# Moving weights placed 64 bytes in front of the stationary operand, modulo 512

## Chip, cores and metric

The kernel runs on one core of one Trainium2 chip. The metric is the device time of one execution in microseconds; lower is better. Before the change three runs took 756.55, 757.05 and 758.76 us, a median of 757.05 us.

## What is computed

The reference is a decoder trunk of two layers over 256 tokens of width 1024, in float32. Layer 0 mixes with a dilated sliding-window attention, layer 1 with a forgetting attention, and each is followed by a SwiGLU feed-forward net (FFN). Cut to what matters here:

```python
h = h + dilated_mixer(rmsnorm(h, g_a), w_in_a, w_out_a)     # w_in: 1024 x 9216, w_out: 1024 x 1024
h = h + swiglu(rmsnorm(h, g_f0), w_gu[0], w_down[0])        # w_gu: 1024 x 5632, w_down: 2816 x 1024
h = h + forgetting_mixer(rmsnorm(h, g_b), w_in_b, b_f, w_out_b)   # w_in: 1024 x 3088
h = h + swiglu(rmsnorm(h, g_f1), w_gu[1], w_down[1])
return rmsnorm(h, g_final)

def swiglu(h, w_gu, w_down):
    gu = h @ w_gu
    g, u = gu[..., :D_FF], gu[..., D_FF:]
    return (silu(g) * u) @ w_down
```

## The kernel before

Each float32 operand of the large products is kept as a pair of rounded float32r parts, high and low (`wh`/`wl` for weights, two halves of `xt` for the normalised activations, `oth`/`otl` for the attention's output, `ah`/`al` for the FFN's gated activations). `mm3` (L179 and L184) makes one product of three matmuls: high times high, high times low, low times high. TensorE keeps one operand still (the stationary one, 128 columns, loaded by LDWEIGHTS) and streams the other (the moving one, 256 or 512 columns). In the profile a matmul row names its operands as output <- moving, stationary, and "128x256" or "128x512" is the moving width.

Weights come as pieces of 128 x 2048. `piece` reads each by two DMAs into `raw` tiles, and `split` writes `wh` by ScalarE (L73) and `wl` by VectorE (L75). Both tags have four buffers in turn. The order of the pieces is the list `order`, and two further pieces are always under way. A piece is used in one of two ways:

- As the stationary operand: `proj_feat`, used for the queries and keys of both mixers (`a_in`, `b_in` with w of 0 or 1) and for the FFN's up projections (`gu`) from f = 3 on. The moving operand is `xt`, 256 columns. One `proj_feat` is 8 steps of `mm3`, so 24 matmuls; one FFN piece (`up(f)`) is 48.
- As the moving operand: `proj_tok` (256 columns; the stationary operand is `xt`) for some values and for the FFN's first three `gu` pieces, the "head" of `ffn`; `proj_pair` (512 columns; `xt` is stationary) for the other values and the very first piece, which is written out in the lead loop (L366); `out_proj` (512 columns; `oth`/`otl` are stationary) with the `a_out` and `b_out` pieces; and `down` (512 columns; `ah`/`al` are stationary) with the `dn` pieces. With `narrow`, `mm3` cuts its second and third matmul into two of 256 columns, so that the next group follows sooner.

In the FFN's main loop two `up(f)` (96 matmuls) alternate with one `down` for both halves of the tokens: 22 matmuls of 512 columns and 4 of 256. One `dn` piece of each layer (f index `LATE`) stands in the tiles of `oth`/`otl` and not in `wh`/`wl`.

Where a tile starts in its partition of SBUF follows from the pools' order and sizes. A `wh` or `wl` buffer has 8192 bytes, 16 times 512, and all other sizes between are such that in the built program every one of them starts at byte 352 modulo 512. A tile of 448 bytes named `gap`, never written, stands ahead of `xt`, which so starts at 288. `ah`, `al`, `oth` and `otl` start at 352. All steps within these tiles that matmuls take are multiples of 512 bytes, so what counts modulo 512 is the same for each matmul of a kind:

| moving <- stationary | where | matmuls | moving minus stationary, modulo 512 |
|---|---|---|---|
| `xt` <- `wh`/`wl`, 256 wide | `proj_feat` | 3360 | -64 |
| `wh`/`wl` <- `xt`, 256 wide | `proj_tok`, narrow ends of `proj_pair` | 500 | +64 |
| `wh`/`wl` <- `xt`, 512 wide | `proj_pair`, lead loop | 278 | +64 |
| `wh`/`wl` <- `oth`/`otl`, 512 wide | `out_proj` | 192 | 0 |
| `wh`/`wl` <- `ah`/`al`, 512 wide | `down` | 438 | 0 |
| `wh`/`wl` <- `ah`/`al`, 256 wide | narrow ends of `down` | 84 | 0 |
| `oth`/`otl` <- `ah`/`al` | `down` of the piece `LATE` | 52 | 0 |

The matmuls are counted in the built program; the offsets are worked out from its addresses.

Of the kernel before, what the change touches and what calls it, by code (L numbers as in the profile page):

```python
# [11 lines left out]
F32R = mybir.dt.float32r  # L12
# [4 lines left out]
P = 128  # L17
# [14 lines left out]
def trunk(ctx: ExitStack, tc: tile.TileContext, T, out):  # L32
    nc = tc.nc

    cst = ctx.enter_context(tc.tile_pool(name="cst", bufs=1))
    wp = ctx.enter_context(tc.tile_pool(name="wp", bufs=1))
# [5 lines left out]
    def first():  # L42

        return tc.high_priority(offset=300)
# [25 lines left out]
    def split(pair, view, src, early=True, after=None):  # L70
        hi, lo = pair
        with first() if early else nullcontext():
            a = nc.scalar.activation(view(hi), src, AF.Copy)  # L73
            with tc.issue_after(after.ins) if after else nullcontext():
                return a, nc.vector.tensor_tensor(view(lo), src, view(hi).bitcast(F32), op=ALU.subtract)  # L75


    def piece(key, todo=None):
        if key[0][:2] == "dn" and key[1] == LATE:
            wh, wl = (y.rearrange("p k c -> p (k c)") for y in fm_tile("ot", KT, 1))  # L80
        else:
            wh, wl = (wp.tile([P, 2048], F32R, tag=y, name=y, bufs=4) for y in ("wh", "wl"))
        for c in range(2):
            raw = wp.tile([P, 1024], F32, tag="raw", name="raw", bufs=5)
            u = slice(c * 1024, (c + 1) * 1024)
            nc.sync.dma_start(raw, T[key[0]][key[1]][:, u])
            cut = lambda after=None, raw=raw, u=u: split((wh, wl), lambda y: y[:, u], raw, False, after)
            if todo is None:
                cut()
            else:  # L90
                todo.append(cut)
        return wh, wl

    def fm_tile(tag, n, bufs):
        return tuple(ap.tile([P, n, S], F32R, tag=f"{tag}{x}", name=f"{tag}{x}", bufs=bufs) for x in "hl")
# [34 lines left out]
    def weights(nm, i, after=None):  # L130

        upto = order.index((nm, i)) + AHEAD
        while state["next"] <= min(upto, len(order) - 1):
            key = order[state["next"]]
            cuts = []
            ready[key] = piece(key, cuts)
            for cut in cuts:
                cut(after)
            state["next"] += 1
        return ready.pop((nm, i))  # L140
# [187 lines left out]
    def in_order(cut):  # L328

        after = ExitStack()  # L330
        for y in cut:
            after.enter_context(tc.issue_after(y.ins))
        return after
# [6 lines left out]
    def square(i):  # L340
        return nc.scalar.activation(part[i].rearrange("p (j s) -> p j s", s=S), xs[i], AF.Square, scale=D ** -0.5)

    def plus(a, b):
        return nc.vector.tensor_tensor(a, a, b, op=ALU.add)

    cut = []
    for k in range(KT):
        if k % 4 == 0:
            w = tuple(wp.tile([P, 2048], F32R, tag=y, name=y, bufs=4) for y in ("wh", "wl"))
        g, u = g_a[:, k:k + 1], slice(k % 4 * 512, k % 4 * 512 + 512)  # L350
        with first(), in_order(cut):
            if k == 0:
                a = nc.vector.tensor_scalar(hi[:, k], xk[k], g, None, op0=ALU.mult)
            else:
                a = nc.scalar.activation(hi[:, k], xk[k], AF.Copy, scale=g)
            b = nc.vector.scalar_tensor_tensor(lo[:, k], xk[k], g, hi[:, k].bitcast(F32), op0=ALU.mult,
                                               op1=ALU.subtract)
            with in_order((a, b)):
                cut = split(w, lambda y: y[:, u], wk[k])
        if k in (1, 5, 7):  # L360
            with first(), in_order(cut):
                a = [square(i) for i in {1: (0, 1), 5: (2,), 7: (3,)}[k]][-1]
                cut = (a, plus(part[0], part[1]) if k == 1 else cut[1])
        for y, z in ((0, 0), (1, 0), (0, 1)):
            for t in range(2):
                nc.tensor.matmul(lead[t], xt[y][:, k, t * P:(t + 1) * P], w[z][:, u], start=k + y + z == 0,  # L366
                                 stop=k == KT - 1 and z == 1)
    cuts = []
    ready[order[1]] = w
    ready[order[2]] = piece(order[2], cuts)  # L370
    ready[order[3]] = piece(order[3], cuts)
    state["next"] = 4
    with first(), in_order(cut):
# [682 lines left out]
```

## Time and profile before

| | |
|---|---|
| runs | 756.55, 757.05, 758.76 us; median 757.05 us |
| profiled execution | span 757.5 us from its first to its last instruction; what lies around the span is not listed for it |
| PE (TensorE's matmuls) busy | 747.3 us, 99% |
| PEld (weight loads, beside PE) busy | 689.3 us, 91% |
| DVE (VectorE) busy | 500.0 us, 66% |
| ACT (ScalarE) busy | 381.7 us, 50% |
| POOL (GpSimd) busy | 56.9 us, 8% |
| mean granted TensorE clock | 0.998 |

The duration that the profile gives a matmul holds its way through the array; the next matmul starts long before it is over. How fast matmuls follow each other is read from the timeline, as the time from a matmul's start to that of the next, or over a stretch as the difference of two starts divided by the number of matmuls between. A stretch of equal matmuls without a wait in it gives the pace of that kind.

### The profile page before, as it was taken

The page shows a single profiled execution, that of the slowest core. Times are in us where ns is not written, and L with a number is a line of the kernel's source. Part 1 is how long each engine was busy: PE and PEld are TensorE (multiplying, and loading weights), DVE is VectorE, ACT ScalarE, POOL GpSimd, SP SyncE. Part 2 cuts the span into 40 slices and gives each one's busy share as a digit, 9 for nine tenths or more (in the row PEclk, how much of TensorE's full clock was granted, in tenths as well). Part 3 has the DMA queues.
Part 4 walks back from the last instruction along what each step waited for, and adds up shares of the span by engine and source line. Part 5 has one row for each costly group of instructions (what it writes and reads, how often), then busy time and mean ns, then how long its engine had stood idle before and what let it go on. Part 6 is the DMA issues. An engine that isn't in the chain of part 4 may idle for free.

```text
span 757.5 us, 14562 instructions
## 1 busy us (share of the span) xinstructions
PE 747.3 (99%) x6018; PEld 689.3 (91%) x6018; DVE 500.0 (66%) x760; ACT 381.7 (50%) x628; POOL 56.9 (8%) x99
## 2 busy tenths in 40 slices
PE   9999999999999999999999999999999999999996
PEld 7998989999988899999999988999889999999995
DVE  7987977877878466545456473887756645456533
ACT  7635437446346455444454454587645444455521
POOL 0600003004013000000000013000000000000000
PEclk9999999999999999999999999999999999999999
DMA  9965553653655267565667454634326665556601
GB/s 333 301 194 168 167 178 127 206 186 115 195 174 195 77 218 248 178 207 180 196 215 233 135 167 140 223 112 151 129 85 220 225 200 190 192 198 209 209 2 55
DMA packets 38355, 135.04 MB, mean 178 GB/s; under 512 B 4369, under 2 KB 5777, under 8 KB 38289
## 3 DMA queue, kind: packets, MB, share of 16 engines
q1 hardware_dynamic: 38144, 134.01, 53.5%
q8 instruction: 47, 0.77, 0.4%
q14 instruction: 20, 0.16, 0.1%
q10 hardware_dynamic: 144, 0.10, 0.0%
HBM read 133.05 MB, written 1.05 MB: 177 GB/s over the span
## 4 chain that ended last, share of the span: by engine, by line
PE 90%; DMA 2%; ACT 2%; issue 2%; DVE 2%; POOL 1%; SPq 0%; POOLq 0%; DVEq 0%; ACTq 0%
PE ps_mm L184 31%; PE ps_mm L179 16%; PE ps_tr L184 9%; PE ps_sc L184 7%; PE ps_o L184 7%; PE ps_tr L179 5%; PE ps_sc L179 4%; PE ps_o L179 3%; PE ps_o L284 2%; PE ps_tr L273 2%; PE ps_sc L832 1%; ACT wh L73 1%; DMA otl<-in_lead 1%; PE ps_sc L430 1%; PE ps_sc L446 1%
## 5 line engine op out<-in xcount | busy, mean ns | idle before, releaser
L73 ACT ACTIVATE wh<-raw 128x1024 fp32r<-128x1024 f32 x236 | 244.0, 1055 | 245.2 <-PE ps_mm L184 82.8
L75 DVE TENSOR_TENSOR wl<-raw,wh 128x1024 fp32r<-128x1024 f32 x236 | 285.4, 1228 | 91.3 <-ACT wh L73 91.0
L179 PE MATMUL ps_mm<-xt,wh 128*128 128x256 f32 x816 | 228.4, 280 | 1.2 <-ACT wh L73 1.2
L184 PE MATMUL ps_mm<-xt,wl 128*128 128x256 f32 x816 | 226.1, 277 | 0.0
L184 PE MATMUL ps_mm<-xt,wh 128*128 128x256 f32 x816 | 226.1, 277 | 0.0
L179 PEld LDWEIGHTS ps_mm<-xt,wh 128*128 128x128 f32 x816 | 153.4, 188 | 4.3 <-issue 2.7
L184 PEld LDWEIGHTS ps_mm<-xt,wl 128*128 128x128 f32 x816 | 153.5, 188 | 0.0
L184 PEld LDWEIGHTS ps_mm<-xt,wh 128*128 128x128 f32 x816 | 153.4, 188 | 0.1
L184 PE MATMUL ps_tr<-xt,wh 128*128 128x256 f32 x304 | 83.8, 276 | 0.0
L184 PE MATMUL ps_tr<-xt,wl 128*128 128x256 f32 x304 | 83.8, 276 | 0.0
L179 PE MATMUL ps_tr<-xt,wh 128*128 128x256 f32 x304 | 83.6, 276 | 0.0
L673 DVE TENSOR_TENSOR sa<-ps_tr,sa 128x256 f32<-128x256 f32 x38 | 16.1, 424 | 73.9 <-PE ps_tr L184 73.9
L184 PEld LDWEIGHTS ps_tr<-xt,wh 128*128 128x128 f32 x304 | 57.1, 188 | 0.0
L184 PEld LDWEIGHTS ps_tr<-xt,wl 128*128 128x128 f32 x304 | 57.1, 188 | 0.0
L179 PEld LDWEIGHTS ps_tr<-xt,wh 128*128 128x128 f32 x304 | 56.9, 188 | 0.0
L179 PE MATMUL ps_mm<-wh,xt 128*128 128x256 f32 (+1 forms) x160 | 52.9, 331 | 0.0
L184 PE MATMUL ps_mm<-wh,xt 128*128 128x256 f32 (+1 forms) x164 | 51.9, 321 | 0.0
L184 PE MATMUL ps_mm<-wl,xt 128*128 128x256 f32 (+1 forms) x164 | 51.9, 320 | 0.0
L259 POOL COPY v<-v 32x256 f32<-32x256 f32 x64 | 33.0, 516 | 138.9 <-ACT v L255 136.1
L149 POOL TENSOR_SCALAR rs<-ssq 128x1 f32<-128x1 f32 x7 | 2.2, 318 | 423.8 <-ACT junk L158 423.8
L184 PEld LDWEIGHTS ps_mm<-wl,xt 128*128 128x128 f32 x164 | 30.8, 188 | 2.6
L184 PEld LDWEIGHTS ps_mm<-wh,xt 128*128 128x128 f32 x164 | 30.5, 188 | 2.9 <-DVE xt L75 0.3
(228 smaller groups left out, 1154.1 us busy)
## 6 DMA issues: line engine op xcount, KB each, us to landing
raw<-in_gu SPq DMA_DIRECT2D x88, 512.0 KB, 4.5
raw<-in_a_in SPq DMA_DIRECT2D x68, 512.0 KB, 4.3
raw<-in_dn SPq DMA_DIRECT2D x44, 512.0 KB, 4.3
raw<-in_b_in SPq DMA_DIRECT2D x24, 512.0 KB, 4.7
raw<-in_a_out SPq DMA_DIRECT2D x8, 512.0 KB, 4.3
raw<-in_b_out SPq DMA_DIRECT2D x8, 512.0 KB, 4.7
grow<-in_norms SPq DMA_DIRECT2D x4, 512.0 KB, 5.4
x<-in_x SPq DMA_DIRECT2D x2, 512.0 KB, 5.6
```

The lines of the kernel that those rows point to most:

```text
L73: a = nc.scalar.activation(view(hi), src, AF.Copy)
L75: return a, nc.vector.tensor_tensor(view(lo), src, view(hi).bitcast(F32), op=ALU.subtract)
L149: nc.gpsimd.tensor_scalar(m, s, rest, None, op0=ALU.add)
L179: nc.tensor.matmul(o, sh, mh, start=start, stop=False)
L184: last = nc.tensor.matmul(o[:, u], s, m[:, u], start=False, stop=end and u.stop == n)
L259: nc.gpsimd.tensor_copy(v[1 + a % 2][n:n + 32, a // 2 * S:a // 2 * S + S], by_t[a * 32:a * 32 + 32, t, g])
L273: nc.tensor.transpose(tr[:, i * P:(i + 1) * P], b, ident)
L284: nc.tensor.matmul(o[h * HD:(h + 1) * HD], v[:, c:c + HD], w(h), start=start, stop=stop)
L430: nc.tensor.matmul(scs[h][:, qb * P:qb * P + (qb + 1) * P], q[hr[h], pr, qb * P:(qb + 1) * P], k[hr[h], pr, :(qb + 1) * P], start=True, st ...
L446: nc.tensor.matmul(sc[h][c, o:o + 64], q[hr[h], pq, qb * P + a * 32:qb * P + a * 32 + 32], k[hr[h], pq].rearrange("p (b n) -> p b n", b=2) ...
L673: nc.vector.tensor_tensor(a, u, sg, op=ALU.mult)
L832: last = nc.tensor.matmul(scs[h][:, qb * P:qb * P + (qb + 1) * P], qz[h][rows[h], pr, qb * P:(qb + 1) * P], kz[h][rows[h], pr, :(qb + 1) * ...
```

## The change

Every `wh` and `wl` tile becomes 2176 elements wide, 512 bytes more, and a piece uses 2048 of them from an offset that depends on how it is used. Pieces whose weights are stationary start at 0 as before. Pieces that move against `xt` (`proj_tok`, `proj_pair`, the first three `gu` pieces, the lead loop) start 96 elements, 384 bytes, in: byte 352 + 384 is 224 modulo 512, which is 288 - 64. Pieces that move against `oth`, `otl`, `ah` or `al` (`a_out`, `b_out`, `dn`) start 112 elements, 448 bytes, in: 352 + 448 is 288 modulo 512, which is 352 - 64. The `LATE` piece is left as it was.

The eight wider tiles need 4096 bytes more in each partition. They come from the scratch area at the start of SBUF that is set aside for DMA descriptors, which is cut from 16384 to 2048 bytes. All other tiles move with that, by 14336 bytes (those ahead of the weights) or 10240 bytes (those behind), both multiples of 512, so no other offset modulo 512 changes. In the built programs the instructions of each engine are the same in number, order, shape and waits.

```diff
+    def shift(key):
+
+        nm, i = key
+        if nm[:2] == "dn" or nm[2:] == "out":
+            return 112
+        return 96 if (i % 3 == 2 if nm[2:] == "in" else i < 3) else 0
+
     def piece(key, todo=None):
         if key[0][:2] == "dn" and key[1] == LATE:
             wh, wl = (y.rearrange("p k c -> p (k c)") for y in fm_tile("ot", KT, 1))
         else:
-            wh, wl = (wp.tile([P, 2048], F32R, tag=y, name=y, bufs=4) for y in ("wh", "wl"))
+            at = shift(key)
+            wh, wl = (wp.tile([P, 2176], F32R, tag=y, name=y, bufs=4)[:, at:at + 2048] for y in ("wh", "wl"))
...
         if k % 4 == 0:
-            w = tuple(wp.tile([P, 2048], F32R, tag=y, name=y, bufs=4) for y in ("wh", "wl"))
+            w = tuple(wp.tile([P, 2176], F32R, tag=y, name=y, bufs=4)[:, 96:96 + 2048] for y in ("wh", "wl"))
...
-    nc = _bacc.Bacc("TRN2", target_bir_lowering=False, num_devices=1)
+    nc = _bacc.Bacc("TRN2", target_bir_lowering=False, num_devices=1, dynamic_dma_scratch_size=2048)
```

## The prediction, made before the changed kernel was run

> **What bounds the kernel now.** I read the busy shares first, then the chain that ended last, then what TensorE waits for, and after that the pace of its matmuls, stretch by stretch.
>
> ```profile
> PE 747.3 (99%) x6018; PEld 689.3 (91%) x6018; DVE 500.0 (66%) x760; ACT 381.7 (50%) x628; POOL 56.9 (8%) x99
> DVE  7987977877878466545456473887756645456533
> PEclk9999999999999999999999999999999999999999
> PE 90%; DMA 2%; ACT 2%; issue 2%; DVE 2%; POOL 1%; SPq 0%; POOLq 0%; DVEq 0%; ACTq 0%
> PE ps_mm L184 31%; PE ps_mm L179 16%; PE ps_tr L184 9%; PE ps_sc L184 7%; PE ps_o L184 7%; PE ps_tr L179 5%; PE ps_sc L179 4%; PE ps_o L179 3%; PE ps_o L284 2%; PE ps_tr L273 2%; PE ps_sc L832 1%; ACT wh L73 1%; DMA otl<-in_lead 1%; PE ps_sc L430 1%; PE ps_sc L446 1%
> ```
> ```profile
> PE ps_mm L179 <- ACT wh L73: 1.2, 1, 1.2
> PE ps_o L293 <- POOL euler L68: 0.9, 1, 0.9
> PE ps_sc L832 <- ACT z L902: 0.6, 1, 0.6
> ```
>
> TensorE is busy 99% of the span at an even granted clock, holds 90% of the chain, and waits 2.7 us in all. So a nanosecond per matmul is a nanosecond of the run. A busy PE need not be at its best pace, so I compare the kinds by operand placement. First the durations:
>
> ```profile
> L184 PE MATMUL ps_tr<-xt,wh 128*128 128x256 f32 x304 | 83.8, 276 | 0.0
> L179 PE MATMUL ps_mm<-wh,xt 128*128 128x256 f32 x96 | 27.2, 283 | 0.0
> L184 PE MATMUL ps_o<-wh,al 128*128 128x256 f32 x32 | 6.4, 283 | 0.0
> L184 PE MATMUL ps_o<-wl,ah 128*128 128x512 f32 x62 | 24.1, 389 | 0.0
> L184 PE MATMUL ps_mm<-wh,xt 128*128 128x512 f32 x60 | 23.6, 393 | 0.0
> ```
>
> Among 256-wide matmuls the one whose moving operand lies 64 bytes in front (`xt` against weights) takes 276 ns; 64 bytes behind (weights against `xt`) 283, and level (weights against `al`) 283. Among 512-wide ones, level takes 389 and behind 393. Shapes, clock and types are equal; what differs is where the operands lie. The pace says how much that is worth. Each pair of rows below is the first matmul of an unbroken stretch and the first row after it (in the pair from 55.31, its last matmul).
>
> In front, 256 wide: 96 matmuls in a feed-forward net, then 144 in the first mixer.
> ```profile
> 290.90 0.29 PE L179 MATMUL ps_mm<-xt,wh 128*128 128x256 f32 x1
> ...
> 301.80 0.39 PE L179 MATMUL ps_sc<-wh,ah 128*128 128x512 f32 x1
> ...
> 179.22 0.28 PE L179 MATMUL ps_mm<-xt,wh 128*128 128x256 f32 x1
> ...
> 196.18 0.38 PE L273 MATMUL ps_tr<-ident,p 128*128 128x128 f32 x2
> ```
> Behind, 256 wide: 54 at the head of a net, then 50 before `out_proj`.
> ```profile
> 266.49 0.28 PE L179 MATMUL ps_o<-wh,xt 128*128 128x256 f32 x1
> ...
> 272.86 0.27 PE L172 MATMUL ps_tr<-ident,xn 128*128 128x128 f32 x1
> ...
> 232.49 0.28 PE L184 MATMUL ps_mm<-wh,xt 128*128 128x256 f32 x1
> ...
> 238.15 0.40 PE L179 MATMUL ps_sc<-wh,oth 128*128 128x512 f32 x1
> ```
> Behind, 512 wide: 22 steps. Level, 512 wide: 30. Level, 256 wide: 4, then 11 in the last product.
> ```profile
> 55.31 0.39 PE L184 MATMUL ps_o<-wl,xt 128*128 128x512 f32 x1
> ...
> 60.35 0.40 PE L184 MATMUL ps_o<-wh,xt 128*128 128x512 f32 x1
> ...
> 441.01 0.39 PE L179 MATMUL ps_sc<-wh,ah 128*128 128x512 f32 x1
> ...
> 447.82 0.27 PE L172 MATMUL ps_tr<-ident,xn 128*128 128x128 f32 x1
> ...
> 306.81 0.40 PE L184 MATMUL ps_o<-wl,ah 128*128 128x256 f32 x2
> ...
> 307.28 0.29 PE L179 MATMUL ps_mm<-xt,wh 128*128 128x256 f32 x1
> 307.40 0.28 PE L184 MATMUL ps_mm<-xt,wh 128*128 128x256 f32 x1
> 307.52 0.28 PE L184 MATMUL ps_mm<-xt,wl 128*128 128x256 f32 x1
> 307.64 0.28 PE L179 MATMUL ps_mm<-xt,wh 128*128 128x256 f32 x1
> ...
> 748.60 0.28 PE L179 MATMUL ps_mm<-wh,ah 128*128 128x256 f32 x1
> ...
> 749.92 0.28 PE L184 MATMUL ps_tr<-wh,al 128*128 128x256 f32 x1
> ```
>
> The paces: in front 10.90/96 = 113.5 ns, but 16.96/144 = 117.8 in the other stretch. Behind 6.37/54 = 118.0, but 5.66/50 = 113.2 in the other. Level, 256 wide: 1.32/11 = 120.0. 512 wide: behind 5.04/22 = 229.1, level 6.81/30 = 227.0. Twice 113.3 is 226.6, so 113.3 ns per 256 columns looks like the floor here, and level at 512 is on it. A slow and a quick pace both occur in front and behind at 256; a stretch that has settled keeps its pace. So the placement sets how likely the slow pace is, and does not forbid it. That is the weak point of what follows.
>
> The likely cause is the weight load that runs beside each matmul:
> ```profile
> 301.81 0.19 PEld L184 LDWEIGHTS ps_sc<-wl,ah 128*128 128x128 f32 x1
> ```
> The matmul of 301.80 is running when, 0.01 us later, the load for the next one starts. It reads the stationary tile while the moving one is read. If they meet in the same part of a 512-byte period, one steps aside for some nanoseconds.
>
> **The change part by part.** No instruction is added, removed or reordered; the sum is matmul counts (from the built program) times differences of pace, all on PE.
>
> 1. Moving weights against `xt`, 256 wide, 500 matmuls, from behind to in front. At 118.0 - 113.5 = 4.5 ns each it is 2.25 us at most; nothing if they keep the slow pace. The stretch from 232.49 is already quick, and some that move will settle slow as that from 179.22 does, so I take two thirds: 1.5 us.
> 2. Moving weights against `xt`, 512 wide, 278 matmuls. In front at 512 columns is in no row of this trace. The nearest rows are behind at 229.1 and in front at 256, which doubled is 227.0. I take the second, since it has the same offset: 278 x 2.1 = 0.6 us. The ends are a gain of 0.7 (the floor, 226.6) and a loss of 278 x 4.0 = 1.1 (the floor with a slip as large as at 256 level, 120.0 - 113.5 = 6.5 ns, which is 233.1).
> 3. `down` and `out_proj`, 512 wide, 630 matmuls, from level to in front. Level has a settled pace of 227.0 and takes a few matmuls to reach it: 301.80 to 306.81 is 22 in 5.01 us, 227.7 each. The gain is at most 630 x 1.1 = 0.7 us down to the floor of 226.6; I take 0.5. The loss, if 512 wide in front costs what 512 wide behind does, is 630 x 1.4 = 0.9 us, and at 233.1 it is 630 x 5.4 = 3.4 us.
> 4. `down`, 256 wide, 84 matmuls: 120.0 to 113.5 in the last product, 0.47/4 = 117.5 in the loop. 84 x 4 to 6.5 is 0.3 to 0.5 us; I take 0.4.
> 5. The up projections after each `down` are not moved themselves, but they start with three matmuls in 0.36 us where the settled pace is 0.34. Some 18 such places (nine in each layer, one after each `down` of the loop) give 0.4 us at most; I take 0.3, since now both sides lie in front.
> 6. Elsewhere: all other tiles move by multiples of 512 bytes. The cut scratch costs nothing as I see it, since 134.01 of 135 MB went over a queue that the profile lists as of a hardware kind:
> ```profile
> q1 hardware_dynamic: 38144, 134.01, 53.5%
> ```
> The writers of the moved tiles are covered by TensorE's own work, as it waited for one of them 1.2 us in the whole run; were that cover gone, one half piece late would cost its length:
> ```profile
> L73 ACT ACTIVATE wh<-raw 128x1024 fp32r<-128x1024 f32 x236 | 244.0, 1055 | 245.2 <-PE ps_mm L184 82.8
> L75 DVE TENSOR_TENSOR wl<-raw,wh 128x1024 fp32r<-128x1024 f32 x236 | 285.4, 1228 | 91.3 <-ACT wh L73 91.0
> ```
> At the head of each net and around the forget gates the chain, in order of time, leaves TensorE though TensorE is busy:
> ```profile
> 278.92 2.01 ACT wh L73 x2
> ...
> 468.19 5.44 POOL gates L797
> ...
> 477.05 6.07 DMA raw<-in_b_in
> ```
> A quicker TensorE will wait there for what it now just meets, and I take 0.2 us off.
>
> Sum: 1.5 + 0.6 + 0.5 + 0.4 + 0.3 - 0.2 = 3.1 us. The profiled span of 757.5 is 0.4 above the median of 757.05, a difference that the spread of the runs (756.55 to 758.76) covers, so I carry the sum over: 757.05 - 3.1 = 753.95, told as 754.0.
>
> The Trainium skill speaks against any gain here. "TensorE: Matmul & The Clock Gate", section "Step-by-step: what each phase is for", says that TensorE has two independent read ports into SBUF and that loading the next tile's weights takes no read bandwidth from the running matmul. By that rule the sum is 0. The rows above (113.5 against 120.0 at equal shape) speak for an interaction of some sort, and that page of the Trainium skill says nothing on placement. What its rule would give stands below as rival C.
>
> **The rivals.**
>
> A. *512-wide matmuls dislike being in front.* For it: at 256 level is the worst (120.0) and at 512 the best (227.0), so a good offset at one width need not be good at the other. Against it: nothing but the doubled 113.5. If they take the 229.1 of behind, part 2 is 0 and part 3 a loss of 0.9: 1.5 + 0 - 0.9 + 0.4 + 0.3 - 0.2 = 1.1 us, 755.9. At 233.1 parts 2 and 3 lose 1.1 and 3.4: the sum is a loss of 2.5, 759.6. The other parts make 2.0 us; with the 908 matmuls of parts 2 and 3 at a pace of 230.3 ns these are eaten up, and above it the change loses.
>
> B. *The up projections settle slow.* Now they enter from level matmuls and reach the quick pace within three. The stretch from 179.22 was entered from moving weights that ran quickly, and settled slow. If entry from weights in front does that in the feed-forward nets, each of the 1824 up matmuls in the two main loops costs 117.8 - 113.5 = 4.3 ns: 7.8 us, less the 3.1 of the sum: 761.8. The point from which it decides: with four in ten of the rounds slow, the gain is gone. Against it: the 304 triples of `ps_tr`, the second half of each round's up projections, average 276 ns, so that no round settles slow now.
>
> C. *No interaction, or the change does nothing.* Both paces occur at both offsets; a state that the offsets do not choose would leave 757.05. Against it: 283 against 276 ns as means over whole groups.
>
> D. *The gain is taken back by waits*, at the three places of the chain above or in the first slices of the page, where VectorE is busy for seven to nine tenths. Some 1.3 us more lost than the 0.2 taken: 755.3.
>
> **How the numbers follow.** 0.3% of 757.05, about what a measurement of this kernel can tell from no change, is 2.3 us: faster is below 754.8, slower above 759.3. My forecast has 0.46, with an own range of 752.5 to 755.0, from part 1 at 2.25 with the others at their upper ends to part 1 at a third; 0.02 of it falls above 754.8. A has 0.17 in its mild form (755.9, same) and 0.10 in its heavy form (759.6, slower). B has 0.12, of which 0.07 for most rounds (slower) and 0.05 for some (same). C has 0.08 and D 0.07, both the same. That gives faster 0.44, same 0.02 + 0.17 + 0.05 + 0.08 + 0.07 = 0.39, slower 0.17. The range reaches from 752.2, a little beyond the upper ends of all parts, to 760.0; it leaves out B for most rounds, the upper part of A's heavy form and a gain above 4.9.
>
> **What would show it.** In the changed kernel the 256-wide matmuls of weights against `xt` should fall from the 283 ns of the group shown to near 276, the narrow ones of `down` from 283 to 276, and 512-wide ones against `xt` from 393 to 389. The stretch from 266.49 should take 6.1 us for its 54 matmuls, not 6.4. A main-loop round (two `up` and one `down`, 290.90 to 307.28, 16.38 us) should take about 16.3. If the 512-wide durations of `down` rise from 389 to 392 or more, A is right; if a round's 96 up matmuls take 11.3 us, B; if all of these stay, C; if they fall and the waits of TensorE grow from 2.7 us, D. The forecast would be wrong above all because 512 wide in front was never seen.

## The result: slower by half a per cent, and the profile after

The changed kernel takes 761.63 us (median of five runs, 760.77 to 761.83), the kernel before 756.78 us (756.55 to 758.76). The ratio is 1.0055, with a 95% interval of 1.0043 to 1.0066: slower, above the 760.0 at which the predicted range ended. Timed again later, each kernel in the same rounds as the other, it was 761.38 against 757.60, a ratio of 1.0052 [1.0040, 1.0064].

The page of the changed kernel first, then the three longest of TensorE's waits, then groups of matmuls by line and shape (busy time, mean ns of one).

```profile
span 759.8 us, 14562 instructions
PE 750.4 (99%) x6018; PEld 687.7 (91%) x6018; DVE 500.0 (66%) x760; ACT 381.5 (50%) x628; POOL 56.1 (7%) x99
PEclk9999999999999999999999999999999999999999
```
```profile
PE ps_o L301 <- POOL euler L68: 0.9, 1, 0.9
PE ps_mm L187 <- DVE qk L422: 0.5, 1, 0.5
PE ps_tr L718 <- DVE sa L666: 0.5, 2, 0.2
```
```profile
L187 PE MATMUL ps_mm<-wh,xt 128*128 128x256 f32 x96 | 27.1, 283 | 0.0
L192 PE MATMUL ps_o<-wl,ah 128*128 128x512 f32 x62 | 24.5, 396 | 0.0
L192 PE MATMUL ps_mm<-wh,xt 128*128 128x512 f32 x60 | 23.8, 397 | 0.0
L192 PE MATMUL ps_o<-wh,al 128*128 128x256 f32 x32 | 6.2, 276 | 0.0
```

TensorE stays the bound: its busy time grew by 3.1 us at the same granted clock (0.998), and its waits came to 2.1 us in place of 2.7. The two 512-wide groups rose, from 389 to 396 ns and from 393 to 397; the narrow ends of `down` fell from 283 to 276 as forecast; the 256-wide group against `xt` stayed at 283, but it mixes values of the mixers with the heads of the nets, and the pace tells these apart.

The timeline gives the pace. In pairs, first row of a stretch and first row behind it: 22 matmuls of `down` in the main loop, with the first `up` of the round and of the next around them; 30 of `down` at the end of the first net; the 54 at that net's head; and one round's 96 `up` matmuls in the second net.

```profile
291.24 0.28 PE L187 MATMUL ps_mm<-xt,wh 128*128 128x256 f32 x1
...
302.12 0.39 PE L187 MATMUL ps_sc<-wh,ah 128*128 128x512 f32 x1
...
307.25 0.39 PE L192 MATMUL ps_o<-wl,ah 128*128 128x256 f32 x2
...
307.71 0.28 PE L187 MATMUL ps_mm<-xt,wh 128*128 128x256 f32 x1
...
442.00 0.39 PE L187 MATMUL ps_sc<-wh,ah 128*128 128x512 f32 x1
...
449.00 0.38 PE L180 MATMUL ps_tr<-ident,xn 128*128 128x128 f32 x2
...
267.18 0.28 PE L187 MATMUL ps_o<-wh,xt 128*128 128x256 f32 x1
...
273.32 0.27 PE L180 MATMUL ps_tr<-ident,xn 128*128 128x128 f32 x1
...
592.90 0.28 PE L187 MATMUL ps_mm<-xt,wh 128*128 128x256 f32 x1
...
604.21 0.40 PE L187 MATMUL ps_sc<-wh,ah 128*128 128x512 f32 x1
```

`down`, 512 wide and in front: 5.13/22 = 233.2 ns in the loop and 7.00/30 = 233.3 at the end, where it was 227.4 (from unrounded starts; the prediction's two rounded rows gave 227.7) and 227.0. Up projections: 10.88/96 = 113.3, quick from the first matmul on; but in the round from 592.90 they take 11.31/96 = 117.8. The head falls from 118.0 to 6.14/54 = 113.7. A whole round took 16.38 us and now takes 16.47.

The quickest settled paces seen are 113.33 ns for 256 columns and 226.67 for 512; they are called the floor here, the time above it the excess, and a matmul that takes longer is said to slip. The excess summed over the whole trace, from the starts of all matmuls (steps over 150 or 245 ns, which hold waits or a change of kind, are left out):

| kind | before, us | after, us | difference | predicted |
|---|---|---|---|---|
| 256 wide, weights against `xt` | 1.83 | 0.71 | -1.1 | -1.5 |
| 512 wide, weights against `xt` | 0.71 | 1.70 | +1.0 | -0.6 |
| 512 wide, `down` and `out_proj` | 0.65 | 4.02 | +3.4 | -0.5 |
| 256 wide, narrow ends of `down` | 0.41 | 0.11 | -0.3 | -0.4 |
| 256 wide, `xt` against weights | 2.62 | 2.52 | -0.1 | -0.3 |

That is +2.8 us from unrounded sums; from the first matmul's start to the last one's it is 749.05 against 751.49, +2.4. The medians lie 3.8 to 4.9 apart. The profiled execution of before explains the difference between the two figures: in the later runs, for which both numbers are known, a run's time is its span plus 1.8 us (761.63 with 759.8 here), so the span of 757.5 belongs to some 759.3 us, above all five of its runs here (756.55 to 758.76).

### The profile page after: what moved, and what is told of

Read it like the earlier page. It is cut to its first block, busy times and chain, and to the rows that moved or that the text cites. A ratio compares the mean times of both kernels' runs of the same rounds, so it can differ in the third digit from the quotient of the medians.

```text
span 759.8 us, 14562 instructions
## 1 busy us (share of the span) xinstructions
PE 750.4 (99%) x6018; PEld 687.7 (91%) x6018; DVE 500.0 (66%) x760; ACT 381.5 (50%) x628; POOL 56.1 (7%) x99
## 4 chain that ended last, share of the span: by engine, by line
PE 90%; DMA 3%; ACT 2%; issue 2%; DVE 1%; POOL 1%; SPq 0%; POOLq 0%; ACTq 0%; DVEq 0%
PE ps_mm L192 30%; PE ps_mm L187 16%; PE ps_tr L192 9%; PE ps_sc L192 8%; PE ps_o L192 7%; PE ps_tr L187 5%; PE ps_sc L187 4%; PE ps_o L187 3%; PE ps_o L292 2%; PE ps_tr L281 2%; PE ps_sc L840 1%; ACT wh L73 1%; DMA otl<-in_lead 1%; PE ps_sc L438 1%; PE ps_sc L454 1%
```

## The experiments

All have the wider tiles and the cut scratch. Most vary `shift`, in elements of 4 bytes, and set the slice of the lead loop, not shown in the cuts, to go with it; the others change what their cut shows. "Level", "in front" and "behind" are offsets 0, -64 and +64 bytes of the moving operand from the stationary one. The first four shared a set of runs, with the kernel before at 758.54 us.

**Room alone.** The wide tiles and the small scratch, nothing moved.

```diff
     def shift(key):
+        return 0
```

> The wider weight tiles and the smaller scratch area alone, every piece at offset 0, so that all placements modulo 512 are those of before. Theory (512-wide matmuls whose moving operand lies 64 bytes in front slip once each, about 233.3 ns instead of 226.7): no change, 756.8 within 1 us, 512-wide durations at 389 to 393 ns as before. Rival (the room itself costs, by the scratch or the moved tiles): 759 to 761.

758.59 us, ratio 1.0002 [0.9993, 1.0011]. Room and scratch cost nothing; all that follows is the offsets.

**Part 1 alone: 256-wide against `xt` in front.**

```diff
+        return 96 if (nm == "a_in" and i in (20, 29) or nm == "b_in" and i in (8, 11) or nm[:2] == "gu" and i < 3) else 0
```

> Only the 480 matmuls of 256 columns of proj_tok are put in front; all 512-wide ones stay as before. Theory: their mean over the floor of 113.3 falls from 3.8 to about 1.5 ns, so 1.1 us faster than before, about 755.7; 512-wide as before. Rival (what the 256-wide gain is taken back by the up projections or by waits): 756.8 or more.

758.19 us, ratio 0.9997 [0.9988, 1.0006]: no gain. The excess of this kind stayed at 1.89 us. The head of the first net in this kernel's timeline, 54 matmuls:

```profile
265.98 0.28 PE L185 MATMUL ps_o<-wh,xt 128*128 128x256 f32 x1
...
272.34 0.38 PE L178 MATMUL ps_tr<-ident,xn 128*128 128x128 f32 x2
```

6.36/54 = 117.8 ns, in front and slow, where the changed kernel with the same operands in the same places has 113.7. The stretch of 52 before the first `out_proj`, quick when behind, went to 117.5; 144 query and key matmuls of the first mixer, themselves unmoved, fell from 117.8 to 113.4. So at 256 columns moving this operand did not choose the pace.

**Part 3 alone: `down` and `out_proj` in front.**

```diff
+        return 112 if nm[:2] == "dn" or nm[2:] == "out" else 0
```

> Only down and out_proj are put in front (630 matmuls of 512 columns, 84 of 256). Theory: 512-wide from about 227.7 to 233.3 ns, 3.4 us lost; 256-wide ends and the start of the next up projections gain 0.3 each; together 2.8 us slower than before, about 759.6. Rival (the loss is that of the whole run's state or of the pieces against xt): within 1 us of before, 512-wide at 389 ns.

761.13 us, ratio 1.0045 [1.0032, 1.0059]. Excess of `down` 2.80 us (6.5 ns each), of `out_proj` 1.17. Part 3 alone makes most of the loss, as theory 1 had it. The heads, behind, stayed at 117.8 although they are now entered from the same slipping `out_proj` as in the changed kernel. Together with the kernel above this says that the heads need both to be quick: the placement and the entry, that is, what runs just before.

**Mixed: 256-wide against `xt` in front, all 512-wide level.**

```diff
+        if nm[2:] == "in" and i % 3 == 2:
+            return 96 if (nm, i) in (("a_in", 20), ("a_in", 29), ("b_in", 8), ("b_in", 11)) else 112
+        return 96 if nm[:2] == "gu" and i < 3 else 0
```

> Each width where it was best so far: 256-wide against xt in front, 512-wide against xt level (offset 0 modulo 512) and down and out_proj level as before. Theory: 512-wide against xt from about 229.3 to about 227.7, 0.5 us, with 1.1 us of the 256-wide ones: 755.2. Rival (level is good only against ah, al, oth, otl, or xt is slow for another reason): 755.7 or more, with 512-wide against xt at 393 ns as before.

757.96 us, ratio 0.9997 [0.9988, 1.0006]. The 512-wide against `xt`, level, have 0.53 us above the floor in place of 0.71 and 1.70, the right sign; the rest of the expected gain did not come, as the 256-wide ones stayed at 1.66, heads at 117.8. The weights of the 512-wide values stand at byte 288 modulo 512 here, as those of `down` do in the changed kernel; against `xt`, level, they settle at the floor, 226.7 ns, and against `ah` and `al` at 233.5. So it is the distance to the partner that counts, and not the weights' own place.

**Sweep of the `down` pieces.** Each of sixteen has its own offset.

```diff
+        at = {"dn0": (16, 32, 48, 64, 80, 96, 104, 120, 0, 0, 0), "dn1": (8, 24, 40, 56, 72, 88, 100, 124, 0, 0, 0)}
+        return at[nm][i] if nm in at else 0
```

> All weights as in the kernel before except that each of the sixteen down pieces of the main loops has an offset of its own, so that its moving operand lies 32 to 496 bytes past the stationary one modulo 512 (128, 64, 192 and so on, 64 and its multiples in the first net, other multiples of 32 or 16 in the second). Theory 1, the slip needs the two operands near each other and the moving one ahead: only offsets just below 512 (480, 496, like 448 before) give 233.3 ns per 512-wide matmul, all others 226.7. Theory 2, the slip is a matter of a 64- or 128-byte part of the period: some contiguous window of offsets slips, the rest does not. Theory 3, any offset other than 0 slips at 512 columns, those of 64 or more only in part: 229 ns for most. The up projections after a slipping down should start at 113.3 ns at once, those after a level or quick one with three slow matmuls, in all three. As a whole within 2 us of the kernel before unless theory 3 holds, which gives +1 to +2 us.

**Sweep of the `up` pieces**, in pairs, with the moving `xt` fixed; the heads are moved too.

```diff
+        at = {"gu0": (32, 16, 32, 48, 64, 80, 96, 112, 104, 8, 0), "gu1": (64, 4, 24, 40, 56, 72, 88, 100, 120, 124, 0)}
+        return at[nm][(i - 1) // 2 if i > 2 else 0] if nm in at else 0
```

> All weights as in the kernel before except that each pair of up pieces has an offset of its own: the moving activations lie 0 to 480 bytes past the stationary weights modulo 512, and the heads of the two nets (256-wide weights against the activations) lie 192 and 320 past. Theory 1, the pace of 256-wide matmuls is set by what precedes them: all pairs start alike, with three slow matmuls after the level down, and settle at 113.3 ns whatever the offset. Theory 2, offset decides: offsets of a window near 0 take 118 to 120 ns (level took 120.0 before), a pair at such an offset costs 0.5 to 0.6 us of its 10.9, and some window far from 0 has no slow start. Heads: theory 1 leaves 117.8 ns, theory 2 gives 113.3 and a gain of 0.58 us each.

762.97 and 766.71 us, one run each, with the kernel before at 758.51. Rows of the first sweep: 22 matmuls of `down` at offset 256, then at 416.

```profile
334.76 0.39 PE L186 MATMUL ps_sc<-wh,ah 128*128 128x512 f32 x1
...
339.76 0.40 PE L191 MATMUL ps_o<-wl,ah 128*128 128x256 f32 x2
...
384.42 0.40 PE L186 MATMUL ps_sc<-wh,ah 128*128 128x512 f32 x1
...
389.57 0.39 PE L191 MATMUL ps_o<-wl,ah 128*128 128x256 f32 x2
```

The second row's 0.39 or 0.40 is of two matmuls that the view joins; only its start counts. 5.00/22 = 227.3 ns at 256 and 5.15/22 = 234.1 at 416 (32 bytes beyond the -64 of the changed kernel). Rows of the second sweep, 96 up matmuls at offset 256, then at 192:

```profile
323.80 0.28 PE L186 MATMUL ps_mm<-xt,wh 128*128 128x256 f32 x1
...
335.29 0.39 PE L186 MATMUL ps_sc<-wh,ah 128*128 128x512 f32 x1
...
340.80 0.29 PE L186 MATMUL ps_mm<-xt,wh 128*128 128x256 f32 x1
...
351.69 0.39 PE L186 MATMUL ps_sc<-wh,ah 128*128 128x512 f32 x1
```

11.49/96 = 119.7 and 10.89/96 = 113.4 (113.5 from the unrounded starts). All offsets in bytes, moving minus stationary; each cell has the pace at the offset and at the offset plus 256 (ns per matmul, from unrounded starts, over 22 steps of `down` or 96 of `up`; 32 and 64 at 512 columns over 15, 416 at 256 over 49; of the 512-wide, 0 is the kernel before and 448 the changed one; of the 256-wide, 448 is the kernel before). Each is one stretch of one execution:

| offset, and + 256 | 512 wide, `down` | 256 wide, `up` |
|---|---|---|
| 0, 256 | 227.4, 227.3 | 119.7, 119.7 |
| 32, 288 | 233.5, 233.4 | 116.7, 116.7 |
| 64, 320 | 228.9, 229.6 | 117.7, 117.7 |
| 96, 352 | 233.6, 233.6 | 120.0, 120.0 |
| 128, 384 | 233.4, 232.5 | 118.7, 118.7 |
| 160, 416 | 234.1, 234.1 | 118.7, 118.8 |
| 192, 448 | 233.6, 233.1 | 113.5, 113.5 |
| 224, 480 | 232.9, 232.8 | 118.3, 118.3 |

Two things stand out. The pattern repeats after 256 bytes, not 512: offsets 256 apart agree within 0.2 ns in thirteen of the sixteen pairs, and within 0.9 in all. And each width has one offset of eight within a nanosecond of the floor, a different one: 0 for 512 columns, 192 (which is -64) for 256. No theory on record said so; theory 3 of the first sweep, that any offset but 0 slips at 512 columns, came nearest, and theory 2 of the second, that the offset decides, held in the main for the up projections. Offsets between the rows go no better: 400 and 496 took 233.3 and 235.5 ns at 512 columns, 48 and 432 took 116.7 and 118.7 at 256. The heads, at 192 and at 320, stayed at 117.8, as theory 1 of the second sweep expected for them: an offset that lets the up projections run at 113.5 does not make a head quick.

The first sweep shows entries as well. After `down` at 0, 64, 96, 160, 192, 256, 352, 384, 400 and 416 the up projections ran at 113.3 to 113.6 ns, after `down` at 32, 128, 224, 288, 320, 480 and 496 at 117.8, all of their 96 matmuls. What an entry does is no matter of 256 bytes, then: 64 and 320 differ, and so do 128 and 384 (one stretch each).

**One part of the activations moved.** `al` 64 bytes up in the first net, `ah` in the second.

```diff
-                acts[f // 2] = tuple(p_tile(512, F32R, f"a{y}") for y in "hl")
+                acts[f // 2] = tuple(p_tile(640, F32R, f"a{y}")[:, 16 * (y == "hl"[1 - l]):][:, :512] for y in "hl")
```

> All weights as in the kernel before; in the first net the low part of the gated activations (al, stationary) is moved 64 bytes up, in the second the high part (ah), so that the weights lie 64 bytes in front of that part and level with the other. Each product is three matmuls: ah with wh, ah with wl, al with wh. Theory 1, the slip belongs to the operands that the matmul itself uses: in the first net one of three slips (al with wh, 233.3 ns; mean 228.9), in the second two of three (both with ah; mean 231.1). Theory 2, the slip comes from the load of the next stationary operand beside the running matmul: in the first net one of three, but ah with wl (the one before al); in the second two of three, ah with wh and al with wh (the ones before ah). The two differ in which of the three is long, not in the time: about 219 x 2.2 + 219 x 4.4 ns = 1.5 us more than before in both. Rival: only an in-front position of both parts matters, then no change.

767.80 us, one run, against 758.51: +9.3 where 1.5 was expected. The first net's `down`, high-high, high-low, low-high and the next:

```profile
304.10 0.39 PE L184 MATMUL ps_sc<-wh,ah 128*128 128x512 f32 x1
304.32 0.39 PE L189 MATMUL ps_sc<-wl,ah 128*128 128x512 f32 x1
304.55 0.40 PE L189 MATMUL ps_sc<-wh,al 128*128 128x512 f32 x1
304.79 0.39 PE L184 MATMUL ps_o<-wh,ah 128*128 128x512 f32 x1
```

The long step is the one of `al` itself (236 ns against 228 and 229), for theory 1, the own operands, and against theory 2, the next load. But in the second net's main loop low times high, level with its own operand, was the longest (234.8 ns in the mean), with high times high at 233.8 and high times low at 231.4, which is the pattern of theory 2. Each theory fits one net and neither both. The surprise lies elsewhere: the up projections, not moved, ran at 117.8 ns in 17 of the 18 stretches that follow a `down`, and their excess rose from 2.6 to 9.8 us. Only what runs before them had changed, and it cost 7.2 us.

**The changed kernel again, and two that aim at the heads.** These and the next shared a set of runs, the kernel before at 757.60.

> The changed kernel once more, timed in the same rounds as the kernel before and the three that follow, so that all stand against one set of runs. If the loss is what the two traces add up to, TensorE's span is 2.4 us longer and the time 2.4 to 3.5 us above the kernel before; if the 4.85 us between the first two medians is all due to the change, it comes out 4.5 to 5.2 us above. The part with only the down and output projections moved was 2.6 us above, so theory 1 (the 512-wide slip is the loss) expects this one 2 to 4 us above.

761.38 us, ratio 1.0052 [1.0040, 1.0064], as told above. Its traced execution had the slow round in the first net and not in the second. The round from 592.90 in the trace shown first, in this one:

```profile
592.92 0.28 PE L187 MATMUL ps_mm<-xt,wh 128*128 128x256 f32 x1
...
603.80 0.39 PE L187 MATMUL ps_sc<-wh,ah 128*128 128x512 f32 x1
```

10.88/96 = 113.3 ns, where the first trace of the same program has 117.8. A stretch of 142 query and key matmuls in the first mixer went the other way, 113.4 ns in the first trace and 117.8 in this one. So the program does not fix the pace of every 256-wide stretch.

Mixed, with the last piece of each output projection in front:

```diff
+        if nm[2:] == "out":
+            return 112 if i == 3 else 0
```

> As the mixed kernel (512-wide against the activations level, down and output projections level, 256-wide against the activations in front), but with the last of the four pieces of each output projection in front, so that the head of each net, itself in front, is entered from slipping matmuls. Theory 1 (the pace of the 256-wide is set by placement and by the state in which it is entered): the heads fall from 117.8 to 113.5 ns as in the changed kernel, 264 x 4.3 = 1.1 us gained, for 48 x 6.6 = 0.3 us lost: 0.8 us below the mixed kernel, 1.3 us below the kernel before. Theory 2 (only placement counts; the quick heads of the changed kernel had another cause): heads stay at 117.8, the time is 0.3 us above the mixed kernel.

The same with the mixers' 256-wide values behind, as before:

```diff
-            return 96 if (nm, i) in (("a_in", 20), ("a_in", 29), ("b_in", 8), ("b_in", 11)) else 112
+            return 0 if (nm, i) in (("a_in", 20), ("a_in", 29), ("b_in", 8), ("b_in", 11)) else 112
```

> As the last, but of the 256-wide pieces against the activations only the heads of the nets are in front; the value pieces of both mixers stay 64 bytes behind as in the kernel before. Theory 1 (state at entry): heads at 113.5 ns as in the last; the 52 matmuls before the first output projection quick again (113.3), the 96 of the second mixer quick again (113.5 in place of 117.7): another 0.2 + 0.4 us gained, 1.9 us below the kernel before. Theory 2: heads at 117.8 and no more than 0.5 us below the kernel before.

757.56 us, 0.9997 [0.9989, 1.0006], and 758.24 us, 1.0009 [1.0000, 1.0018]. The head of the first of the two:

```profile
266.22 0.28 PE L189 MATMUL ps_o<-wh,xt 128*128 128x256 f32 x1
...
272.35 0.38 PE L182 MATMUL ps_tr<-ident,xn 128*128 128x128 f32 x2
```

6.13/54 = 113.5 ns: all four head stretches of both kernels are quick, on theory 1. The whole is no quicker: stretches in the mixers settled otherwise. The same stretch of 142 is at 117.8 ns in both traces, where the mixed kernel's has 113.4; and in the second kernel the 52 before the first `out_proj` and the 96 of the second mixer stayed at 117.8, though their own offset is again that of the kernel before, with 113.3 and 113.5.

**The failed step by itself: `down` in halves of 256 columns.** Same operands, same places, in front.

```diff
+            for s, m, end in ((sh, mh, False), (sh, ml, False), (sl, mh, stop)):
+                for c in (0, 256):
+                    u = slice(c, c + 256)
+                    last = nc.tensor.matmul(o[:, u], s, m[:, u], start=False, stop=end and c > 0)
```

> The changed kernel, but each 512-wide matmul of a down projection (but for the first of each accumulation) is cut into two of 256 columns with the same operands in the same places. This is the step of the prediction that took 512 wide in front for twice 256 wide in front. Theory 1 (the same offset is good for 256 and bad for 512 columns): in front each half takes 113.3 ns, a pair 226.7 in place of 233.3; some 370 pairs gain 2.4 us, the 44 of the late piece, which is level, take 240 in place of 227 and lose 0.6: 1.8 us below the changed kernel. Theory 2 (the slip comes from these operands in front, at any width): each half takes 117.8 to 120, a pair 235.6 to 240, and the time is 1.5 to 3 us above the changed kernel.

The same `down` as that from 302.12 above, now 48 matmuls:

```profile
301.31 0.39 PE L192 MATMUL ps_sc<-wh,ah 128*128 128x256 f32 x2
...
306.75 0.28 PE L194 MATMUL ps_mm<-xt,wh 128*128 128x256 f32 x1
```

5.44/48 = 113.3 ns, the floor, twice 113.3 in place of 233.2. Theory 1 is shown: at this offset 512 columns slip and 256 do not. The time is 758.98 us, 2.4 below the changed kernel; the ratio to the kernel before is 1.0041 [1.0017, 1.0066]. Five of its eight times lie at 757.2 to 759.0 and three at 762.9 to 764.4; the next two kernels suggest why.

**All 512-wide matmuls in halves**, `mm3` and the lead loop alike, but for the late piece.

```diff
-    def mm3(o, stat, mov, start, stop, narrow=False):
+    def mm3(o, stat, mov, start, stop, narrow=False, halves=True):
...
+        if halves and n == 512:
```

> The changed kernel with every 512-wide matmul cut into two of 256 columns (down but for the late piece, output projections, values and the lead loop), all in front. With the down projections cut, the remaining 512-wide ones in front had 1.7 us above the floor against the activations and 1.2 us against the attention's output, and the late piece, level and cut, 0.6 us. Theory 1 (256 wide in front runs at 113.3 ns): these fall to some 0.3 us, so TensorE's span is 2.9 us below the kernel with only the down projections cut and 4.2 us below the kernel before: near 753.5 us, a ratio of 0.994 to 0.996. Theory 2 (an entry from halves leaves the 256-wide stretches of the mixers and heads in their slow state, 117.8 ns): 500 to 1000 matmuls more at 4.4 ns, 2 to 4 us given back, a ratio of 0.997 to 1.001. Rival: a quicker TensorE waits for the writers of the weights or its clock is granted lower: then PE's waits or the clock of the run show it, and the ratio is 1.00 or more.

774.30 us, ratio 1.0225 [1.0206, 1.0245]: far from expected. From the waits, then the timeline of one `down` of the first net and one of the second:

```profile
PE ps_tr L180 <- DVE xn L175: 3.3, 2, 2.0
PE ps_tr L561 <- POOL rs_a L412: 2.0, 1, 2.0
```
```profile
306.72 0.40 PE L192 MATMUL ps_sc<-wh,ah 128*128 128x256 f32 x2
...
312.37 0.28 PE L194 MATMUL ps_mm<-xt,wh 128*128 128x256 f32 x1
...
613.67 0.39 PE L192 MATMUL ps_sc<-wh,ah 128*128 128x256 f32 x2
...
619.11 0.28 PE L194 MATMUL ps_mm<-xt,wh 128*128 128x256 f32 x1
```

5.3 us are new waits for the norms, whose cause I did not follow up. Pace makes some 4.2 us more, by the excess of all kinds against the kernel before. The traced execution took 769.98 us, the least of the five; what the others, up to 777.5, spent more is not shown. Equal code at equal offsets takes 5.65/48 = 117.7 ns in the first net and 5.44/48 = 113.3 in the second, and each net keeps its pace through all eight rounds, up projections included.

**Each width at its good offset.** `down` in halves and in front, the late piece level and whole, the other 512-wide level, heads and their entry in front.

```diff
+        if nm[:2] == "dn":
+            return 112
```

> Each width at its good offset: the down projections cut into halves of 256 columns and in front (but for the late piece, level and whole), the 512-wide matmuls of the values, the lead loop and three of the four pieces of each output projection level, the heads of the nets in front with the piece before them in front too. Theory 1, both nets settle quick as with only the down projections cut: against that kernel the 512-wide ones against the activations fall from 1.7 to 0.5 us above the floor, those of the output projections from 1.2 to 0.6, the late piece from 0.6 to 0.1, so TensorE's span is 2.3 us shorter there and 3.6 below the kernel before: 754 us, a ratio of 0.995 to 0.997. Theory 2, the state in which a net is entered is not fixed by the program: some executions have a net of 144-matmul rounds at 117.8 ns, 5.1 us more each, so the times of this kernel stand in groups some 5 us apart, about 754, 759 and 764 us, and the median is no better than the kernel before. The profiled execution shows which state each net had.

762.30 us, ratio 1.0032 [1.0014, 1.0051]. Its twelve times stand in two groups, four at 757.5 to 758.1 and eight at 761.5 to 763.3. The profiled execution, of the upper group, one `down` of each net:

```profile
300.76 0.39 PE L196 MATMUL ps_sc<-wh,ah 128*128 128x256 f32 x2
...
306.20 0.28 PE L198 MATMUL ps_mm<-xt,wh 128*128 128x256 f32 x1
...
601.85 0.40 PE L196 MATMUL ps_sc<-wh,ah 128*128 128x256 f32 x2
...
607.50 0.28 PE L198 MATMUL ps_mm<-xt,wh 128*128 128x256 f32 x1
```

5.44/48 = 113.3 and 5.65/48 = 117.7: here the second net is slow. Its 768 up and 336 `down` matmuls at 4.45 ns are 4.9 us, and the groups' means, 757.7 and 762.7, are 5.0 apart. Theory 2 stands in its main point: the times stand in groups a net's worth apart, so which pace a net takes is not fixed by the program. No execution of the lower group was traced, so that it is the one with both nets quick is inferred from the difference. If it is, the 3.6 us that theory 1 expected below the kernel before shrank to 0.6 (757.7 against 758.25), for a reason that was not followed up. No version here is faster than the kernel before by more than the noise.

## Why the prediction was wrong

**Part 2, the step that failed.** Asked for 512 columns in front, which no row showed, the prediction weighed "behind at 229.1 and in front at 256, which doubled is 227.0" and took "the second, since it has the same offset". A good offset does not carry over from one width to the other: 512 columns in front took 233.3, and the same operands in halves twice 113.3. Part 2 lost 1.0 us where 0.6 was to be gained.

**Part 3** stood on the same step and weighed most: 630 matmuls, +3.4 us against -0.5. The 0.5 was a quickening from 227.0 towards the floor that no 512-wide row of the prediction showed. Its own upper end, "at 233.1 it is 630 x 5.4 = 3.4 us", is what happened. The row that should have decided was in the fence: level is the worst place at 256 columns (120.0) and the best at 512 (227.0), so the offset that is best at 256 had no claim on 512. Rival A said that, at 0.10 for its heavy form, and its 759.6 is 2.0 below the time.

**Part 1** is near in size, -1.1 of -1.5, by luck, and wrong in reason. The placement alone gave nothing (758.19 us with only these moved, heads at 117.8); the heads became quick as they were in front and also entered from an `out_proj` that slips. That slip is the very thing that part 3 had not foreseen; with `out_proj` level, the heads stayed slow. The prediction named the weak point, "a stretch that has settled keeps its pace", and then priced the part by offset.

**Part 4** held (283 to 276 ns, -0.3 us). **Part 5** held in the loop, where the up projections start at 113.3 at once in 15 of the 16 rounds. The sixteenth took that gain of 0.3 us back: rival B in small, in one round where it needed four in ten. The second mixer, with a stretch of 96 at 117.8 (113.5 before), lost 0.5 us, and the first gained 0.7, nearly all of it by the stretch of 142 that the changed kernel's second trace has slow again. So the -0.1 of this kind in the table is largely chance. **Part 6**: TensorE waits no more than before; room and scratch cost nothing. **Rival D**, a gain lost to waits, was not put to the test, as there was no gain to lose.

**Rival C** falls. The Trainium skill, "TensorE: Matmul & The Clock Gate", section "Step-by-step: what each phase is for", has the load of the next weights take no read bandwidth from the running matmul; by that rule placement could not matter. Here equal matmuls at an equal clock took 227.0 or 233.3 ns by placement alone, so the measurement decides against reading it that far. The prediction's "likely cause", the load that meets the moving operand "in the same part of a 512-byte period", is not shown: the period measured is 256 bytes, and of the test with one part moved each theory fits one net.

**The base.** "The profiled span of 757.5 is 0.4 above the median" compared a span with a run's time, which is 1.8 longer. The execution lay some 2 us above the median, so even right differences would have been carried over from an untypical one. That does not change the sign.

The cause was thus narrowed to width, distance and entry, and no further. What stays open: why the two widths differ by 64 bytes in their good offset, and what sets the pace of a 256-wide stretch at its entry.

## What to carry to other kernels

A pace measured at one shape is no price for another, even at the same offset: measure that shape, or carry the other end of the range as an equal. When a stretch can run at two paces, ask what enters it: here, behind the level 512-wide matmuls of `down`, every stretch of up projections of the kernel before came to the quick pace, and without them whole nets could fall to the slow one. One kernel with sixteen offsets showed here what no theory of the period had said.

## What the hardware did that was not expected

- The offset between the two operands counts modulo 256 bytes for the settled pace, to within 0.9 ns in the pairs swept. What a bad offset costs hardly grows with the width: 233.3 - 226.7 = 6.6 ns per 512-wide matmul in front, 120.0 - 113.3 = 6.7 per 256-wide one at level.
- At 256 columns and the good offset two settled paces exist, 113.3 and 117.8 ns. The pace can differ between executions of one program: 117.8 and 113.3 ns over the same round of 96 in the two traces of the changed kernel, and by inference some 5 us over one net in the last one.
